# Gate/up products in five PSUM banks per unit, in another order, with operands moved to 64 modulo 256 bytes

## The chip, the cores and the metric

The kernel runs on one core of one Trainium2 chip. The metric is device time in microseconds (us). The core has a matmul engine (PE, with its weight loads shown as PEld), a vector engine (DVE), a scalar engine (ACT), GpSimd (POOL), and DMA queues, most of them fed by SyncE (SP). Each engine runs its own instructions in order. Matmul results go into PSUM, which has eight banks of 512 fp32 columns on 128 partitions; operands lie in SBUF.

## The reference

One encoder layer on a 1024 x 1024 activation in fp32: a half-step feed-forward network (FFN 1), two attention groups with 8 heads each, a second half-step FFN (FFN 2), and a final norm.

```python
def swiglu(h, w_gu, w_down):                      # w_gu 1024 x 5632, w_down 2816 x 1024
    a, b = jnp.split(h @ w_gu, 2, axis=-1)
    return (jax.nn.silu(a) * b) @ w_down

h = modulate(rms_norm(x, g_ffn1), sh_f1, sc_f1)
x = x + 0.5 * gt_f1 * swiglu(h, w1_gu, w1_down)   # FFN 1
h = modulate(rms_norm(x, g_mix), sh_m, sc_m)
z = h @ w_in                                      # then the two attention groups
x = x + gt_m * (concat(rms_norm(o_mla), rms_norm(o_gqa)) @ w_out)
h = modulate(rms_norm(x, g_ffn2), sh_f2, sc_f2)
x = x + 0.5 * gt_f2 * swiglu(h, w2_gu, w2_down)   # FFN 2
return rms_norm(x, g_final)
```

The shifts, scales and gates come from `silu(c) @ w_ada + b_ada`, nine blocks of 1024.

## The kernel before, in words

Every fp32 operand is split into two parts, high (`h`, rounded) and low (`l`, the remainder), and a product is three matmuls: high by high, low moving operand by high, high by low (lines 484 to 486). One matmul takes a stationary operand of 128 x 128 and a moving one of 128 x 512.

The gate/up product `h @ w_gu` of each FFN is done in 22 units. A unit is a 2 x 2 block product in which seven products stand for eight: A11 B11, A12 B21, S1 T1, S2 T2, S3 T3, S4 B22 and A22 T4. The A and S blocks are made from the weights and are the stationary operands; the B and T blocks are made from the activations, stay in SBUF for the whole stage (`B11h`, `T1l` and so on) and are the moving operands. A product is 12 matmuls (four blocks of depth by three). A profile row such as `ps<-T1h,uh` is the product S1 T1, `B22h` is S4 B22, `T4h` is A22 T4, `B21h` is A12 B21.

The weights come through a stream (class `Stream`, lines 52 to 159): a 1 MB DMA per unit into one of two `raw` buffers, POOL and DVE form S1 to S4 (line 424), then each block is split: ACT copies the high part (`uh`, line 105), DVE subtracts to get the low part (`ul`, line 106). A ring of nine split blocks runs ahead of the products. The order of the splits is the list of steps in `unit_specs`. After every product `tick()` lets the stream do two steps, and every second tick adds one step of the modulation sums (line 311: a DVE instruction on 1024 columns, fed by a 512 KB DMA; rows `acc<-ada,cact,acc`; FFN 1 only).

What follows a product is on DVE and ACT: U2 = A11 B11 + S2 T2 (line 629), U4 = U2 + S1 T1 (line 637), and `post` (lines 494 to 510), which adds what is missing, applies silu on even units, and multiplies on odd ones. POOL forms sums of the results (line 520), and they go to DRAM for the down product.

For units 0 to 7 ("early" units) A11 B11 and A12 B21 are done ahead, and A11 B11 comes back from DRAM as `c1`; only five products remain in `run()`. Units 8 to 21 have all seven.

`run()` takes its PSUM banks by `ps1()`, which goes round six banks in a fixed order (`SIX`). Before, a unit of seven products uses three: `bank[u]` for A11 and A12, `b` for S2, S1 and S4 one after the other, `c` for S3 and A22. S1 is added onto S2 in `b`, so PE may start S1 only when U2 has been read from `b`, and S4 only when U4 has been read. A22 is added onto S3 in `c` after `post(u, 1, 1)` has read `c`. The modulation stage takes banks from the same round: one for a set of columns (line 326), two for a gate (line 340).

A scheduler puts the instructions of each engine in order at build time from its own estimates, and may set matmuls of one product between those of another where it expects a wait.

SBUF is handed out in pools from the left and from the right end. On the right come `rawp`, `tmp`, `sm`, `sp` and then, in FFN 1, the pools R1 and R2 with the B and T blocks. On the left lie the constants, the ring, and in FFN 2 the pools R1b and R2b with the B and T blocks. With the sizes of the pools, the ring's tiles and those of R1b and R2b start at 64 modulo 256 bytes, those of `rawp` and `tmp` at 224, and those of `sp`, R1, R2 and the right-side tiles of the attention (K, Q, V, the probabilities, `hT`) at 96.

Of the kernel before, what the change touches and what calls it, by code (L numbers as in the profile page):

```python
# [15 lines left out]
F32 = mybir.dt.float32  # L16
# [3 lines left out]
ALU = mybir.AluOpType  # L20
# [4 lines left out]
P = 128  # L25
# [26 lines left out]
class Stream:  # L52
# [87 lines left out]
    def get(self, key):  # L140
        while key not in self.units:
            assert self.i <= self.where[key], key
            if self._next_is_block() and self.live >= RING:
                self.live -= self.freed
                self.freed = 0
                assert self.live < RING, key
            self._step()
        return self.units[key]
# [35 lines left out]
def encoder_layer(ctx: ExitStack, tc: tile.TileContext, a: dict, out: bass.AP):  # L184
    nc = tc.nc

    const = ctx.enter_context(tc.tile_pool(name="const", bufs=1))
    ring = ctx.enter_context(tc.tile_pool(name="ring", bufs=RING))
    rawp = ctx.enter_context(tc.tile_pool(name="rawp", bufs=RAWB, side="right"))
    tmp = ctx.enter_context(tc.tile_pool(name="tmp", bufs=6, side="right"))  # L190
    sm = ctx.enter_context(tc.tile_pool(name="sm", bufs=4, side="right"))
# [6 lines left out]
    def tick(n=2):  # L198
        bg.step()
        st.pump(n)  # L200
        ada_ticks[0] += 1
        if ada_ticks[0] % 2 == 0:
            ada.pump(1)
# [8 lines left out]
    def t2(name, dt=F32):  # L212
        return tmp.tile([P, 512], dt, tag="t2", name=name, bufs=6)

    def small(n, name):
        return sm.tile([P, 16], F32, tag="small", name=name, bufs=18)[:, 0:n]

    def mm3(o, ah, al, bh, bl, start, stop):
        nc.tensor.matmul(o, ah, bh, start=start, stop=False)
# [3 lines left out]
    def inv_rms(ss, dims, r):  # L223

        v = small(ss.shape[1], "v")
        if isinstance(dims, int):
            nc.vector.tensor_scalar(v, ss, 1.0 / dims, EPS, op0=ALU.mult, op1=ALU.add)  # L227
        else:
            for i, d in enumerate(dims):
                nc.vector.tensor_scalar(v[:, i:i + 1], ss[:, i:i + 1], 1.0 / d, EPS, op0=ALU.mult, op1=ALU.add)  # L230
        nc.gpsimd.tensor_tensor(r, v, neghalf[:, 0:ss.shape[1]], op=ALU.pow)  # L231
# [40 lines left out]
    def use_banks(kinds):  # L272
        banks.update(kinds=kinds, n=0, pair=None)

    def ps2():
        return p2p.tile([P, 1024], F32, tag="ps2", name="ps2")

    def ps1():

        if banks["pair"] is not None:  # L280
            p = banks["pair"][:, 512:1024]
            banks["pair"] = None
            return p
        kind = banks["kinds"][banks["n"] % len(banks["kinds"])]
        banks["n"] += 1
        if kind[0] == "2":
            p = ps2()
            if kind == "2":
                banks["pair"] = p
            return p[:, 0:512]  # L290
        return (p0p if kind == "0" else p1p).tile([P, 512], F32, tag="ps1", name="ps1")
# [62 lines left out]
    def norm_gen(t, xt, i, hTh=None, hTl=None, hf=None):  # L354

        ss = small(1, "ss")
        sumsq(xt, ss)
        yield
        r = small(1, "r")
        inv_rms(ss, D, r)  # L360
        yield
        xn = t4("xn")
        nc.vector.tensor_scalar(xn, xt, r, None, op0=ALU.mult)
        yield
        c, q = divmod(t, 4)
        qs = slice(q * P, (q + 1) * P)
        p = [ps1().rearrange("p (k q) -> p k q", k=4) for half in range(2)]
        for k in range(KT):
            nc.tensor.transpose(out=p[k // 4][:, k % 4, :], in_=xn[:, k * P:(k + 1) * P], identity=ident)
        h = hf[c][:, :, qs] if hf else t4("h").rearrange("p (k q) -> p k q", k=KT)  # L370
        for k in range(KT):
            nc.scalar.activation(h[:, k, :], p[k // 4][:, k % 4, :], AF.Identity,
                                 scale=modA[i][:, k:k + 1], bias=modB[i][:, k:k + 1])
        if hf:
            return
        yield
        dh = hTh[c][:, :, qs]
        dl = hTl[c][:, :, qs]
        nc.vector.tensor_copy(dh, h)
        nc.vector.tensor_tensor(dl, h, f32(dh), op=ALU.subtract)  # L380
# [33 lines left out]
    def unit_specs(i, u, early):  # L414

        src = a[f"w{i}_gu"][u // 2, u % 2]
        A = [slice(j * 512, (j + 1) * 512) for j in range(4)]
        tmps = {}

        def comb(nm, eng, x, y, op):  # L420
            def f(raw):
                tmps[nm] = sp.tile([P, 512], F32, tag="S", name="S")
                get = lambda v: tmps[v] if isinstance(v, str) else raw[:, A[v]]
                eng.tensor_tensor(tmps[nm], get(x), get(y), op=op)  # L424
            return f

        def blk(nm, v):
            if isinstance(v, str):
                return ((i, u, nm), None, lambda raw: tmps[v])
            return ((i, u, nm), A[v], None)  # L430

        direct = not early
        steps = [comb("S1", nc.gpsimd, 2, 3, ALU.add), comb("S3", nc.gpsimd, 0, 2, ALU.subtract)]
        if direct:
            steps.append(blk("A11", 0))
        steps += [comb("S2", nc.vector, "S1", 0, ALU.subtract), blk("S2", "S2")]
        if direct:
            steps.append(blk("A12", 1))
        steps += [blk("S1", "S1"), blk("S3", "S3"), comb("S4", nc.vector, 1, "S2", ALU.subtract), blk("S4", "S4"),
                  blk("A22", 3)]  # L440
        return [(src, steps)]

    gtp = {}
# [1 line left out]
    class GateUp:  # L445
# [164 lines left out]
        def run(self):  # L610
            use_banks(SIX)
            K4 = (0, 1, 2, 3)
            self.load_p1(0)
            for u in range(NU):
                early = u < NE
                self.load_p1(u + 1)
                if early and u % 2:
                    self.g["A21"] = gtp["g"]()
                    nc.sync.dma_start(self.g["A21"], ge_d[u // 2])
                if not early:  # L620
                    self.bank[u] = ps1()
                    self.prod(self.bank[u], u, "A11", "B11", K4, True, True)
                    self.keep_p1(u)
                    tick()
                c1 = self.c1.pop(u)
                b = ps1()
                self.prod(b, u, "S2", "T2", K4, True, True)
                u2 = t2("U2")
                nc.vector.tensor_tensor(u2, b, c1, op=ALU.add)
                tick()  # L630
                if not early:
                    self.prod(self.bank[u], u, "A12", "B21", K4, False, True)
                    self.post(u, 0, 0, self.bank[u])
                    tick()
                self.prod(b, u, "S1", "T1", K4, False, True)
                u4 = t2("U4")
                nc.vector.tensor_tensor(u4, b, c1, op=ALU.add)
                tick()
                c = ps1()
                self.prod(c, u, "S3", "T3", K4, True, True)  # L640
                self.post(u, 1, 1, c, u4)
                tick()
                self.prod(b, u, "S4", "B22", K4, False, True)
                self.post(u, 0, 1, b, c1)
                tick()
                self.prod(c, u, "A22", "T4", K4, False, True)
                self.post(u, 1, 0, c, u2)
                del self.bank[u]
                tick()

    def gu_specs(i):
        for u in range(NU):
            for src, steps in unit_specs(i, u, "rest" if u < NE else None):
                st.add(src, steps)
# [753 lines left out]
    for s in range(NQ + LAG + 3):  # L1408
# [5 lines left out]
        b = s - LAG  # L1414
        if 0 <= b < NQ:
            g, e = divmod(b, 2)
# [299 lines left out]
```

## Time and profile before

| | us |
|---|---|
| median of 3 runs (2076.69 to 2081.34) | 2081.32 |
| profiled execution | 2080.87 |
| its span, first to last instruction | 2079.1 |
| PE busy | 1989.1 (96%) |
| DVE busy | 1556.7 (75%) |
| ACT busy | 977.0 (47%) |
| POOL busy | 473.6 (23%) |

The stages lie in the span about like this: the start and the early products to 98 us, `run()` of FFN 1 to 537, its down product to 750, projections and attention to 1315, the output projection to 1417, early products and `run()` of FFN 2 to 1859, its down product to the end. A matmul's row shows a duration of about 0.39 us, but matmuls overlap: the pace is the distance from one start to the next. A wait stands in brackets behind the instruction that waited, with its releaser.

### The profile page before, as it was taken

Reading aid. Unit: us, or ns where it says so; the run is one execution under the profiler, and the core shown is the slowest. Engines: PE = TensorE matmul, PEld = TensorE weight load, DVE = VectorE, ACT = ScalarE, POOL = GpSimd, SP = SyncE. Lnnn points to the kernel's source line nnn. Section 1 sums busy time; section 2 is a strip of 40 time slices with the busy share of each in tenths; the row PEclk is TensorE's granted clock in tenths of the full one; section 3 lists DMA queues with packets and bytes.
Section 4 is the critical chain, followed back from the end, with each engine's and each line's share of the span. In section 5 each row is a group of like instructions: output and inputs, shape, how many; then the busy total and the mean of one; then the engine's idle time right before and its main releaser. Section 6 shows DMA issues by size and latency. Waiting matters only on the chain. (4 is left out here: it accounts for less than half of the span.)

```text
span 2079.1 us, 28011 instructions
## 1 busy us (share of the span) xinstructions
PE 1989.1 (96%) x10301; PEld 1678.2 (81%) x10301; DVE 1556.7 (75%) x2381; ACT 977.0 (47%) x1865; POOL 473.6 (23%) x428
## 2 busy tenths in 40 slices
PE   6889999999999999899999999998899999999998
PEld 4667777777788888888989999997678888888886
DVE  7898777775598777588788877776877566656976
ACT  6522222223344473477787777466332333234444
POOL 1533433332100014121220000014444233220011
PEclk9899999999999999999999999999999999999999
DMA  8266654542752342631343332243453233268223
GB/s 339 104 236 202 203 166 157 190 155 101 296 221 92 122 145 90 175 117 58 111 147 102 82 82 62 102 142 127 147 176 136 78 126 103 80 225 332 96 92 117
DMA packets 90550, 303.30 MB, mean 146 GB/s; under 512 B 9848, under 2 KB 22427, under 8 KB 76588
## 3 DMA queue, kind: packets, MB, share of 16 engines
q1 hardware_dynamic: 81018, 274.21, 39.4%
q0 software_dynamic: 7040, 23.07, 2.8%
q10 hardware_dynamic: 2354, 4.22, 0.5%
q8 instruction: 81, 1.33, 0.3%
q14 instruction: 57, 0.47, 0.1%
HBM read 220.98 MB, written 80.49 MB: 145 GB/s over the span
## 5 line engine op out<-in xcount | busy, mean ns | idle before, releaser
L106 DVE TENSOR_TENSOR ul<-raw,uh 128x512 fp32r<-128x512 f32 (+1 forms) x343 | 275.6, 810 | 68.2 <-ACT uh L105 68.0
L105 ACT CAST uh<-raw 128x512 fp32r<-128x512 f32 (+1 forms) x343 | 210.5, 622 | 236.3 <-PE ps L485 165.0
L105 ACT CAST uh<-S 128x512 fp32r<-128x512 f32 x198 | 122.0, 622 | 369.7 <-PE ps L485 277.9
L726 PE MATMUL ps<-uh 128*128 128x512 f32 x616 | 240.6, 391 | 1.1 <-ACT uh L105 1.0
L727 PE MATMUL ps<-ul,uh 128*128 128x512 f32 x616 | 240.2, 390 | 0.6 <-DVE ul L106 0.6
L728 PE MATMUL ps<-uh,ul 128*128 128x512 f32 x616 | 240.0, 390 | 0.0
L1413 DVE TENSOR_REDUCE nm<-ps 128x1 f32<-128x1024 f32 x128 | 155.6, 1215 | 70.3 <-PE ps L221 40.9
L424 POOL TENSOR_TENSOR S<-raw 128x512 f32<-128x512 f32 x88 | 125.7, 1434 | 290.8 <-DVE ul L106 138.9
L106 DVE TENSOR_TENSOR ul<-S,uh 128x512 fp32r<-128x512 f32 x198 | 168.9, 857 | 30.4 <-ACT uh L105 27.6
L520 POOL TENSOR_TENSOR g<-g 128x512 f32<-128x512 f32 x88 | 125.1, 1421 | 221.0 <-DVE g L507 219.6
L1431 ACT CAST ph<-ps 128x512 fp32r<-128x512 f32 x256 | 138.0, 590 | 79.5 <-PE ps L1430 79.3
L1441 DVE TENSOR_TENSOR pl<-ps,ph 128x512 fp32r<-128x512 f32 x256 | 163.9, 682 | 0.0
L1436 ACT ACTIVATE pe<-ps,nm 128x1024 f32<-128x1024 f32 x128 | 143.7, 1123 | 17.0 <-DVE nm L1413 17.0
L726 PEld LDWEIGHTS ps<-uh 128*128 128x128 f32 x616 | 115.7, 188 | 25.9 <-ACT uh L105 2.0
L727 PEld LDWEIGHTS ps<-ul,uh 128*128 128x128 f32 x616 | 115.7, 188 | 25.0 <-DVE ul L106 1.2
L1430 PE MATMUL ps<-ident,pe 128*128 128x128 f32 x1024 | 134.8, 273 | 0.8 <-DVE pl L1441 0.4
L728 PEld LDWEIGHTS ps<-uh,ul 128*128 128x128 f32 x616 | 115.7, 188 | 23.8
L1430 PEld LDWEIGHTS ps<-ident,pe 128*128 128x128 f32 x1024 | 119.6, 140 | 18.9 <-DVE pl L1441 0.6
L1379 PE MATMUL po<-ph,V 128*128 128x256 f32 x512 | 129.5, 291 | 0.0
L1380 PE MATMUL po<-pl,V 128*128 128x256 f32 x512 | 125.7, 284 | 0.0
L105 ACT CAST uh<-hT 128x512 fp32r<-128x512 f32 x96 | 59.7, 622 | 137.4 <-PE ps L727 102.3
L231 POOL TENSOR_TENSOR r<-v,neghalf 128x1 f32<-128x1 f32 x32 | 25.9, 810 | 358.0 <-DVE v L227 358.0
(282 smaller groups left out, 5190.1 us busy)
## 6 DMA issues: line engine op xcount, KB each, us to landing
raw<-in_w_gu_dram SPq DMA_DIRECT2D x52, 1024.0 KB, 4.9
ada<-in_w_ada_dram SPq DMA_DIRECT2D x56, 512.0 KB, 3.6
g_S<-g POOLq DMA_DIRECT2D x88, 256.0 KB, 2.6
g_A<-g SPq DMA_DIRECT2D x66, 256.0 KB, 3.6
hT<-in_w_down_dram SPq DMA_DIRECT2D x16, 1024.0 KB, 10.3
raw<-g_S SPq DMA_DIRECT2D x16, 1024.0 KB, 4.8
raw<-g_A SPq DMA_DIRECT2D x12, 1024.0 KB, 5.0
x<-in_x_dram SPq DMA_DIRECT2D x16, 512.0 KB, 14.9
```

Of the source, the lines that this page charges most:

```text
L105: nc.scalar.copy(hi[:, 0:n], ap)
L106: nc.vector.tensor_tensor(lo[:, 0:n], ap, f32(hi[:, 0:n]), op=ALU.subtract)
L424: eng.tensor_tensor(tmps[nm], get(x), get(y), op=op)
L726: nc.tensor.matmul(p, gh[:, tsl], wh, start=start, stop=False, skip_group_check=True)
L727: nc.tensor.matmul(p, gh[:, tsl], wl, start=False, stop=False, skip_group_check=True)
L728: nc.tensor.matmul(p, gl[:, tsl], wh, start=False, stop=stop, skip_group_check=True)
L1379: nc.tensor.matmul(po[:, 0:256], V, gr.ph[:, k, :], start=(k == 0), stop=False)
L1413: nc.vector.tensor_reduce(nm, p, axis=AX.X, op=ALU.max, negate=True)
L1430: nc.tensor.transpose(out=pt[:, k, :], in_=pe[:, (4 * n + k) * P:(4 * n + k + 1) * P], identity=ident)
L1431: nc.scalar.copy(gr.ph[:, 4 * n:4 * n + 4, es], pt)
L1436: nc.scalar.activation(pe, p, AF.Exp, bias=nm, accum_out=ls[:, s % 2:s % 2 + 1])
L1441: nc.vector.tensor_tensor(gr.pl[:, nsl, es], pts[n], f32(gr.ph[:, nsl, es]), op=ALU.subtract)
```

## The change

1. In `run()` S1, S2 and S4 get a bank each (`e`, `b`, `d`), so a unit of seven uses five banks: `bank[u]` (A11, A12), `b` (S2), `e` (S1), `c` (S3, A22), `d` (S4). U4 is now `e` + U2, and the result of S4 is `d` + U4.
2. The order of the products becomes A11, S2, S1, S3, A12, S4, A22; before it was A11, S2, A12, S1, S3, S4, A22. The splits in `unit_specs` follow. Early units have S2, S1, S3, S4, A22 in both.
3. A pad of 160 bytes at the right end (`padr`, 40 fp32) and two more `small` buffers of 64 bytes. With these the right-side pools `rawp` and `tmp` move by 160 bytes, and `sp` and all behind it by 288. So every SBUF operand of a product starts at 64 modulo 256: 224 - 160 = 64, and 96 - 288 + 256 = 64. The left side stays.

```diff
+    padr = ctx.enter_context(tc.tile_pool(name="padr", bufs=1, side="right"))
+    padr.tile([P, 40], F32, name="padr")
     rawp = ctx.enter_context(tc.tile_pool(name="rawp", bufs=RAWB, side="right"))
...
-        return sm.tile([P, 16], F32, tag="small", name=name, bufs=18)[:, 0:n]
+        return sm.tile([P, 16], F32, tag="small", name=name, bufs=20)[:, 0:n]
...
-        steps += [comb("S2", nc.vector, "S1", 0, ALU.subtract), blk("S2", "S2")]
+        steps += [comb("S2", nc.vector, "S1", 0, ALU.subtract), blk("S2", "S2"), blk("S1", "S1"), blk("S3", "S3")]
         if direct:
             steps.append(blk("A12", 1))
-        steps += [blk("S1", "S1"), blk("S3", "S3"), comb("S4", nc.vector, 1, "S2", ALU.subtract), blk("S4", "S4"),
-                  blk("A22", 3)]
+        steps += [comb("S4", nc.vector, 1, "S2", ALU.subtract), blk("S4", "S4"), blk("A22", 3)]
...
-                if not early:
-                    self.prod(self.bank[u], u, "A12", "B21", K4, False, True)
-                    self.post(u, 0, 0, self.bank[u])
-                    tick()
-                self.prod(b, u, "S1", "T1", K4, False, True)
+                e = ps1()
+                self.prod(e, u, "S1", "T1", K4, True, True)
                 u4 = t2("U4")
-                nc.vector.tensor_tensor(u4, b, c1, op=ALU.add)
+                nc.vector.tensor_tensor(u4, e, u2, op=ALU.add)
                 tick()
                 c = ps1()
                 self.prod(c, u, "S3", "T3", K4, True, True)
                 self.post(u, 1, 1, c, u4)
                 tick()
-                self.prod(b, u, "S4", "B22", K4, False, True)
-                self.post(u, 0, 1, b, c1)
+                if not early:
+                    self.prod(self.bank[u], u, "A12", "B21", K4, False, True)
+                    self.post(u, 0, 0, self.bank[u])
+                    tick()
+                d = ps1()
+                self.prod(d, u, "S4", "B22", K4, True, True)
+                self.post(u, 0, 1, d, u4)
                 tick()
                 self.prod(c, u, "A22", "T4", K4, False, True)
                 self.post(u, 1, 0, c, u2)
```

On PE, at unit 7 (an early one) of FFN 1, before: the end of S2 T2 (into bank `ps_1772`), then the first four matmuls of S3 T3 (into `ps_1814`), then S1 T1, again into `ps_1772`.

```order
L486 MATMUL ps_1772<-T2h_568,ul 128x512
L484 MATMUL ps_1772<-T2h_568,uh 128x512
L485 MATMUL ps_1772<-T2l_569,uh 128x512
L486 MATMUL ps_1772<-T2h_568,ul 128x512
L484 MATMUL ps_1814<-T3h_560,uh 128x512
L485 MATMUL ps_1814<-T3l_561,uh 128x512
L486 MATMUL ps_1814<-T3h_560,ul 128x512
L484 MATMUL ps_1814<-T3h_560,uh 128x512
L484 MATMUL ps_1772<-T1h_556,uh 128x512
```

The same place now: S2 T2 goes into `ps_1790`, S1 T1 into a bank of its own, `ps_1812`.

```order
L485 MATMUL ps_1790<-T2h_572,uh 128x512
L486 MATMUL ps_1790<-T2l_573,uh 128x512
L487 MATMUL ps_1790<-T2h_572,ul 128x512
L485 MATMUL ps_1812<-T1h_560,uh 128x512
L486 MATMUL ps_1812<-T1l_561,uh 128x512
L487 MATMUL ps_1812<-T1h_560,ul 128x512
```

S1 stands directly behind S2, the part of S3 that had been set between them is gone, and the two write to different banks.

On DVE, at unit 11 (odd, with seven products) of FFN 1, before: U2, a result of A12 (line 507 on a PSUM bank), U4, and the result of S3 (line 506 with U4).

```order
L629 TENSOR_TENSOR U_2414<-ps_2401,c_2390 128x512
L106 TENSOR_TENSOR ul<-S,uh 128x512
L507 TENSOR_TENSOR g<-ps_2377,s 128x512
L106 TENSOR_TENSOR ul<-S,uh 128x512
L424 TENSOR_TENSOR S<-S,raw 128x512
L637 TENSOR_TENSOR U_2453<-ps_2401,c_2390 128x512
L106 TENSOR_TENSOR ul<-S,uh 128x512
L424 TENSOR_TENSOR S<-raw,S 128x512
L506 TENSOR_TENSOR g<-ps_2461,U_2453 128x512
```

The same unit now, to the result of A12 (`ps_2403`).

```order
L630 TENSOR_TENSOR U_2440<-ps_2427,c_2416 128x512
L106 TENSOR_TENSOR ul<-S,uh 128x512
L426 TENSOR_TENSOR S<-S,raw 128x512
L635 TENSOR_TENSOR U_2459<-ps_2446,U_2440 128x512
L106 TENSOR_TENSOR ul<-raw,uh 128x512
L507 TENSOR_TENSOR g<-ps_2468,U_2459 128x512
L106 TENSOR_TENSOR ul<-S,uh 128x512
L508 TENSOR_TENSOR g<-g,s 128x512
L426 TENSOR_TENSOR S<-raw,S 128x512
L508 TENSOR_TENSOR g<-ps_2403,s 128x512
```

DVE does the same kinds of instruction; U4 reads its own bank and U2, and the result of A12 comes behind that of S3.

## Rows read from the trace of the kernel before

**Rows 1.** The page, busy time of two engines: us, share of span, instructions.

```profile
PE 1989.1 (96%) x10301; PEld 1678.2 (81%) x10301; DVE 1556.7 (75%) x2381; ACT 977.0 (47%) x1865; POOL 473.6 (23%) x428
```

**Rows 2.** Windows: start:end, length, then busy time of each engine (instructions), clock, DMA.

```profile
core 0: us, PE busy (x) PEld busy (x) DVE busy (x) ACT busy (x) POOL busy (x), PEclk, DMA share, GB/s
98.40:237.60 139.20, 126.48 (x516) 98.84 (x515) 118.18 (x138) 37.31 (x63) 53.36 (x45) 0.95 0.65 215
237.60:470.00 232.40, 220.04 (x945) 173.86 (x944) 181.71 (x209) 65.74 (x110) 83.20 (x74) 0.99 0.52 173
470.00:537.00 67.00, 67.00 (x289) 53.88 (x288) 33.48 (x51) 20.13 (x34) 10.32 (x11) 1.00 0.36 133
1600.00:1700.00 100.00, 100.00 (x443) 82.83 (x442) 61.38 (x84) 32.61 (x54) 31.18 (x29) 1.00 0.27 95
```

**Rows 3.** PE's waits, 98.4 to 237.6: us in total, times, longest.

```profile
PE ps L484 <- DVE U L629: 7.1, 4, 3.2
PE ps L484 <- DVE U L637: 5.2, 2, 3.5
```

**Rows 4.** PE's waits, 237.6 to 470 (all that there are).

```profile
PE ps L484 <- DVE U L637: 7.1, 5, 3.4
PE ps L484 <- DVE U L629: 5.3, 5, 1.7
```

**Rows 5.** Timeline about one wait: start, us, engine, line, operation, tiles.

```profile
291.77 4.16 DVE L311 SCALAR_TENSOR_TENSOR acc<-ada,cact,acc 128x1024 f32<-128x1024 f32 x1
292.28 1.31 POOL L520 TENSOR_TENSOR g<-g 128x512 f32<-128x512 f32 x1
293.53 1.30 POOL L424 TENSOR_TENSOR S<-raw 128x512 f32<-128x512 f32 x1
...
298.25 0.68 DVE L637 TENSOR_TENSOR U<-ps,c 128x512 f32<-128x512 f32 x1
298.98 0.65 PE L484 MATMUL ps<-B22h,uh 128*128 128x512 f32 x1 [3.36 <-DVE U L637]
301.54 0.68 DVE L500 TENSOR_TENSOR s<-ps,U 128x512 f32<-128x512 f32 x1
```

**Rows 6.** Timeline of PE, first and last of gapless stretches in FFN 1.

```profile
472.65 0.40 PE L484 MATMUL ps<-B22h,uh 128*128 128x512 f32 x1
...
534.25 0.40 PE L484 MATMUL ps<-T4h,uh 128*128 128x512 f32 x1
```

**Rows 7.** The same for FFN 2.

```profile
1605.81 0.39 PE L484 MATMUL ps<-B22h,uh 128*128 128x512 f32 x1
...
1796.21 0.39 PE L484 MATMUL ps<-B22h,uh 128*128 128x512 f32 x1
```

**Rows 8.** The same for the input projection, 512 columns.

```profile
787.34 0.40 PE L219 MATMUL ps<-uh,hT 128*128 128x512 f32 x1
...
792.94 0.40 PE L219 MATMUL ps<-uh,hT 128*128 128x512 f32 x1
```

**Rows 9.** DVE groups by line, 98.4 to 237.6: count, busy us, mean ns, idle before.

```profile
L106 DVE TENSOR_TENSOR ul<-S,uh 128x512 fp32r<-128x512 f32 x36 | 30.0, 847 | 0.0
```

**Rows 10.** PE's waits, 1466 to 1592.3, `run()` of FFN 2, early units.

```profile
PE ps L484 <- ACT es L501: 1.8, 1, 1.8
PE ps L484 <- DVE U L629: 1.5, 3, 0.6
```

**Rows 11.** Timeline of PE: scores of one step, and what follows them.

```profile
1216.25 0.40 PE L219 MATMUL ps<-K,Q 96*128 96x512 f32 x1
...
1217.64 0.60 PE L1430 MATMUL ps<-ident,pe 128*128 128x128 f32 x4
```

**Rows 12.** Timeline of PE: probabilities by V, first and last of 13.

```profile
1214.57 0.28 PE L1379 MATMUL po<-ph,V 128*128 128x256 f32 x1
...
1216.01 0.28 PE L1379 MATMUL po<-ph,V 128*128 128x256 f32 x1
```

**Rows 13.** Timeline of PE: output projection, `oth` from the left side, 25 starts.

```profile
1356.57 0.28 PE L219 MATMUL ps<-uh,oth 128*128 128x256 f32 x1
...
1359.45 0.28 PE L219 MATMUL ps<-uh,oth 128*128 128x256 f32 x1
```

## The prediction

> **What bounds the kernel now.** I read the page first. PE is busy 1989.1 of 2079.1 us, DVE 1556.7 [rows 1], so the kernel is paced by PE nearly everywhere, and time can be won in two ways only: matmuls that start closer together, or PE pauses that go. The profiled execution took 2080.87 us, 1.8 us more than its span and 0.45 us less than the median of the runs, so a sum made on it needs no correction.
>
> The windows then show where PE pauses [rows 2]. `run()` of FFN 1 has three stretches. In A, 98.4 to 237.6 us (early units), PE is busy 126.5 of 139.2 us at a mean clock of 0.95. In B, 237.6 to 470, it is 220.0 of 232.4 us at 0.99. In C, 470 to 537, PE is busy throughout, as in the late units of FFN 2 (the window 1600 to 1700). The table of PE's waits gives the cause: in A 7.1 us for U2 (line 629) and 5.2 us for U4 (line 637) [rows 3]; in B 7.1 us for U4 and 5.3 us for U2, and nothing else [rows 4]. These are the two reads of the shared bank `b`. They come where the modulation sums run beside the units: one such sum took 4.16 us while POOL worked, U4 came at 298.25, and S4 waited 3.36 us for it [rows 5]. DVE is busy 118.2 of 139.2 us in A and 181.7 of 232.4 us in B, but 33.5 of 67 us in C [rows 2], where the sums are over.
>
> The third view is the timeline of starts in gapless stretches. In FFN 1, 264 matmuls from 472.65 to 534.25 us make 61.60 / 264 = 233.3 ns from start to start [rows 6]. In FFN 2, 840 from 1605.81 to 1796.21 us make 190.40 / 840 = 226.7 ns [rows 7]. Clock 1.00, shape, line and stationary operand are the same in both; what differs is where the B and T blocks lie: at 96 modulo 256 on the right in FFN 1, at 64 on the left in FFN 2. In the input projection the moving operand (ring) is at 64 and the stationary one (`hT`, right side) at 96: 24 matmuls in 5.60 us, 233.3 ns again [rows 8]. I read this as 6.7 ns per matmul of 512 columns as soon as one of its operands starts at 96.
>
> **The change part by part.** *Operands at 64.* `run()` of FFN 1 has 8 x 60 + 14 x 84 = 480 + 1176 matmuls. The 1176 of B and C save 1176 x 6.67 ns = 7.8 us. Those of A are worth 3.2 us but stand beside a loaded DVE, so they are counted with A below. The 192 early products are worth at most 1.3 us; PE pauses much there, so 0.5. The input projection has 192 matmuls of 512 columns: 1.3 us. The scores have 640 of 512 columns, both operands at 96: six, up to the next instruction, take 1.39 us or 232 ns [rows 11], so 0 to 3.4 us; I take half, 1.7, because the nearest other pair in that stage shows nothing: probabilities by V, 256 columns with both at 96, keep 120 ns [rows 12], and the output projection with both at 64 has 2.88 us / 24 = 120 ns too [rows 13]. Everything else of fewer columns is taken at nothing, with 2 us to either side. FFN 2 and both down products have their operands at 64 already: nothing.
>
> [...] The rows on the starts differ by 6.7 ns, and only the run can say whether by start or by side.
>
> *S1 and S4 in banks of their own, stretch B.* The waits of 7.1 and 5.3 us have no reason left: neither S1 nor S4 touches a bank that was read a moment ago. The slow restart behind a wait goes with them: the mean clock of 0.99 over 232.4 us is 2.3 us. What is late next is A22, which must still find `c` read by `post(u, 1, 1)`. That comes behind U4 on DVE, but in a unit of seven two products (A12, S4, together 5.4 us) now lie between S3 and A22, where before one did. In the worst case of the trace U4 started at 298.25 and the read of `c` at 301.54, done at 302.2 [rows 5]; S3 had ended about 295.6, so A22 would come at 301.0 and wait 1.2 us in place of 3.36. Two such cases make 2 us left. The gate of the modulation takes two banks of the round of six; with five per unit, `d` then falls on `bank[u]`, and S4 waits for the result of A12 just done. By the order this happens twice in B; DVE reads such a bank in 0.68 us [rows 5] behind one or two others, so about 1 us each, 2 us (0 to 5). B and C together: 7.8 + 12.4 + 2.3 - 2 - 2 = 18.5 us saved (13 to 22.5).
>
> *Stretch A.* The early units have no A12 between S2 and S1, so before S1 waits for U2 in any case; now it follows at once. But DVE becomes the limit: it is busy 118.2 us there [rows 2], with 36 splits of S blocks at 847 ns [rows 9] where an undisturbed DVE instruction of this size takes 0.68 us [rows 5]. The change takes nothing from DVE (U4 reads one bank and one SBUF tile, as before). PE's own work is 516 x 0.2267 = 117 us. So A can't fall below about 120 us, and two engines that are both nearly full, with only S4 between S3 and A22 as slack, do not reach that. I take 127, a gain of 12 us, between 3 (only the alignment comes through) and 19.
>
> [...]
>
> *FFN 2, early units.* U2 is waited for 1.5 us, and ACT 1.8 us [rows 10]; the latter stays. With the restarts I take 2 us (1 to 3).
>
> *More splits in another order.* The steps of the stream follow the products, the same number on the same engines; the ring keeps its lead of nine blocks, which hides it (PE waits for no split in A and B [rows 3, 4]). If that lead were used up, PE would wait for `ul`, up to 0.85 us a block.
>
> Sum: 18.5 (B, C) + 12 (A) + 2 (FFN 2) + 1.3 (input projection) + 1.7 (scores) + 0.5 (early products) = 36.0 us. 2080.87 - 36.0 = 2044.9, so 2045.
>
> **The rivals.** *First: it is the side, not the start.* In the trace all operands at 96 lie in right-side pools and all of FFN 2's at 64 on the left, so the 6.7 ns may belong to the place or to something of FFN 1. Then the pad buys nothing: B and C lose 7.8, A some 3, and 3.5 of projection, scores and early products go: 36.0 - 14.3 = 21.7 us, 2059. For it: both pools of 96 are on the right, and the scores, with both operands at 96, run no slower than those with one. Against it: in the input projection it is the other operand that lies at 96, and the pace is the same to 0.1 ns.
>
> *Second: the waits move to A22.* DVE is late by the same amount, and PE meets it one or two products further on. Then A keeps only its 3 us, B and C keep 7.8 and a third of 14.7, FFN 2 has 1, the rest 3.5: 20 us, 2061. For it: in A the slack is one product, and DVE is 85% busy. Against it: A22 does not appear among the waits now, and in B its slack doubles.
>
> *Third, slower: A22 waits in every unit.* `post(u, 1, 1)` stands behind U4 and up to three splits and combinations on DVE; were it late by over 5.4 us (2.7 in early units) in all 44 units of both FFNs, A22 would wait each time. The gain is eaten when that wait is 36.0 / 44 = 0.8 us a unit on average; at 1.2 us it makes 2098. Against it: in FFN 2's late units and in C nothing waits at all, with less slack.
>
> *Fourth: hardly any effect*, if the alignment is the side's and DVE paces all of A and B as before: 2077 or so.
>
> **How the numbers follow.** The forecast has 0.57, with a range of its own of 2030 to 2058: A at 120, B and C at 22.5, the scores at 3.4 and the small ones at their best give 51 us or 2030; A at 132 (7), B and C at 13, FFN 2 at 1 and the scores at 0 give 23 us or 2058. The first rival has 0.2, the second 0.15, the third 0.03, the fourth 0.05. The range of 2028 to 2066 takes in the first two, and 2 us for the matmuls of fewer columns. A measurement of this kernel tells 0.3%, 6.2 us, from no change: faster by more has 0.57 + 0.2 + 0.15 = 0.92, within has 0.05, slower 0.03.
>
> **What would show it.** Right: starts 226.7 ns apart in FFN 1's `run()` and in the input projection's 512-column part, no wait for U2 or U4 left in the table of PE's waits, A near 127 us with DVE over 90% busy, a few waits on the read of `c` (tile `T4h`) or of `bank[u]` (tile `B22h`) in A and B. Wrong: 233 ns in FFN 1 (first rival); `T4h` waits that sum to ten us or more (second); PE pauses in FFN 2's late units, where there are none (third); or slower matmuls of 128 or 256 columns in the attention.

## The result, and the profile after

The changed kernel took 2058.15 us (median of 4 runs, 2051.58 to 2059.17), the kernel before on the same chip 2081.33 (2076.69 to 2083.57). The ratio is 0.9881, 95% interval 0.9870 to 0.9893: faster, by 23 us where 36 were forecast. The span of the profiled execution is 2056.6 us against 2079.1. By stage, each from its first matmul to the first of the next; FFN 2's early products (51.8 and 51.7 us) and the 2.7 us of transpositions between attention and output projection are left out:

| stage | before, us | after, us | difference | forecast |
|---|---|---|---|---|
| FFN 1, early products | 74.7 | 73.5 | -1.2 | -0.5 |
| FFN 1, `run()`, stretch A | 138.9 | 132.0 | -6.9 | -12 |
| FFN 1, `run()`, B and C | 299.4 | 279.7 | -19.7 | -18.5 |
| FFN 1, down product | 216.9 | 220.6 | +3.8 | 0 |
| input projection | 123.8 | 121.7 | -2.1 | -1.3 |
| attention | 434.2 | 434.5 | +0.3 | -1.7 |
| output projection | 102.8 | 103.7 | +0.8 | 0 |
| FFN 2, `run()` | 389.5 | 386.7 | -2.8 | -2 |
| FFN 2, down product | 220.3 | 225.9 | +5.6 | 0 |

The windows of the same three stretches, which answer to [rows 2]; the columns are the same:

```profile
97.30:229.30 132.00, 121.81 (x512) 98.11 (x513) 119.74 (x137) 37.37 (x63) 54.12 (x44) 0.95 0.65 219
229.30:442.00 212.70, 210.37 (x943) 172.76 (x943) 179.00 (x210) 62.51 (x108) 81.34 (x71) 1.00 0.56 190
442.00:509.00 67.00, 66.73 (x292) 54.40 (x290) 31.83 (x46) 17.94 (x32) 13.97 (x15) 1.00 0.31 113
```

In B, PE now pauses 2.3 us in place of 12.4, and DVE's share rose to 84%. In A, DVE is busy 119.7 of 132 us, as long as before: the stretch became shorter and DVE had the same to do.

PE's waits in A, and below the dots all of those in B, answer to [rows 3, 4]: us in total, times, longest.

```profile
PE ps L485 <- DVE s L501: 9.4, 3, 5.0
PE ps L485 <- POOL acc L310: 3.5, 1, 3.5
PE ps L485 <- DVE g L507: 0.7, 1, 0.7
...
PE ps L485 <- DVE s L501: 1.8, 3, 1.0
PE ps L485 <- DVE g L507: 0.5, 1, 0.5
```

No wait for U2 or U4 is left. The one for `acc` is the pause ahead of the first product of `run()` (S2 T2, begun at 97.32 us) and is over before A begins. That GpSimd ended it is not certain: the splits of that product were made in the same microsecond. All the others are at A22 (`T4h`), at the reads of `c`, most of them at `s` of line 501, the read by `post(u, 1, 1)`, which A22 must follow. They sum to 12.4 us, 10.1 of them in A, where PE's pauses thus fell from 12.7 only to 10.2 us; the rest of A's gain, 4.4 us, is PE's own busy time. The longest of these waits in the timeline, to be laid beside [rows 5]:

```profile
142.74 2.77 DVE L313 SCALAR_TENSOR_TENSOR acc<-ada,cact,acc 128x1024 f32<-128x1024 f32 x1
...
145.43 0.68 DVE L635 TENSOR_TENSOR U<-ps,U 128x512 f32<-128x512 f32 x1
...
146.03 0.68 DVE L106 TENSOR_TENSOR ul<-S,uh 128x512 fp32r<-128x512 f32 x1
146.63 0.68 DVE L426 TENSOR_TENSOR S<-raw,S 128x512 f32<-128x512 f32 x1
147.23 0.68 DVE L501 TENSOR_TENSOR s<-ps,U 128x512 f32<-128x512 f32 x1
...
148.06 0.76 PE L485 MATMUL ps<-T4h,uh 128*128 128x512 f32 x1 [5.00 <-DVE s L501]
```

A modulation sum of 2.77 us, then U4, a split, a combination, and only then the read of `c`; A22 (`T4h`) stood for 5.0 us. It is the case of [rows 5], with another product at its end.

The starts in FFN 1 without a gap, which answer to [rows 6]:

```profile
448.73 0.39 PE L485 MATMUL ps<-T4h,uh 128*128 128x512 f32 x1
...
472.30 0.39 PE L487 MATMUL ps<-B11h,ul 128*128 128x512 f32 x1
```

The two starts are 104 matmuls apart: 23.57 us / 104 = 226.6 ns, where there were 233.3. In the input projection's 512-column part, the starts without a gap are 227.2 ns apart on the mean, against 233.3.

The new loss lies at the head of both down products. SyncE's queue there, before (the first four rows) and after:

```profile
526.04 0.81 SPq L714 DMA_DIRECT2D hT<-in_w_down_dram  x2
...
540.47 0.39 SPq L95 DMA_DIRECT2D raw<-g_A  x1
...
553.56 0.32 SPq L395 DMA_DIRECT2D gate<-gd  x1
...
556.05 0.98 SPq L95 DMA_DIRECT2D raw<-g_A  x2
```

```profile
502.06 0.32 SPq L517 DMA_DIRECT2D g_A<-g  x1
503.32 0.81 SPq L717 DMA_DIRECT2D hT<-in_w_down_dram  x2
...
521.41 0.33 SPq L397 DMA_DIRECT2D gate<-gd  x1
521.78 1.95 SPq L978 DMA_DIRECT2D x<-in_x_dram  x4
523.84 0.97 SPq L95 DMA_DIRECT2D raw<-g_A  x2
```

The down product starts at 537.05 before and at 509.04 after. Its first `w_down` load went out 11.0 us ahead of it, and now 5.7. The third chunk of `g_A12` (`raw`) went out 3.4 us behind its start, ahead of the gate row; now it goes 14.8 us behind, after the gate row (which waits 9.3 us for the last `g_S` store to leave its place) and four loads of x. ACT and PE then show the price (after):

```profile
532.92 0.62 ACT L105 CAST uh<-raw 128x512 fp32r<-128x512 f32 x1 [11.18 <-DMA raw<-g_A]
```

```profile
534.11 0.50 PE L729 MATMUL ps<-uh 128*128 128x512 f32 x1 [1.92 <-ACT uh L105]
534.92 0.50 PE L730 MATMUL ps<-ul,uh 128*128 128x512 f32 x1 [0.31 <-DVE ul L106]
...
1857.19 0.79 PE L729 MATMUL ps<-uh 128*128 128x512 f32 x1 [3.31 <-ACT uh L105]
```

```profile
531.00:541.00 10.00, 7.77 (x26) 5.67 (x25) 6.80 (x11) 5.92 (x11) 0.00 (x0) 0.83 0.91 350
1853.00:1863.00 10.00, 6.68 (x22) 4.74 (x22) 6.12 (x10) 5.92 (x11) 0.00 (x0) 0.83 0.82 319
```

PE stands for 1.9 and 3.3 us, and the mean granted clock over these ten us is 0.83; windows of one us show 0.50 from 537 to 539 and from 1858 to 1860, and 1.00 from 540 and from 1861 on. Added up over the starts of each stretch, what exceeds 227 ns a matmul is 4.4 and 5.5 us, so pause, late second operand and lower clock together cost more than the pause. Another 1.2 us go in the first five us of each down product. The first down product of before has a pause of its own, 1.9 us with its restart, at 568 us.

### The profile page after: what moved, and what is told of

It reads as the page before. It is cut to its first block, busy times and chain, and to the rows that moved or that the text cites. A ratio compares the mean times of both kernels' runs of the same rounds, so it can differ in the third digit from the quotient of the medians.

```text
span 2056.6 us, 28024 instructions
## 1 busy us (share of the span) xinstructions
PE 1974.8 (96%) x10301; PEld 1678.4 (82%) x10301; DVE 1570.0 (76%) x2381; ACT 973.6 (47%) x1865; POOL 473.5 (23%) x428
## 5 line engine op out<-in xcount | busy, mean ns | idle before, releaser
L106 DVE TENSOR_TENSOR ul<-raw,uh 128x512 fp32r<-128x512 f32 (+1 forms) x343 | 255.0, 749 | 42.6 <-ACT uh L105 42.3
L106 DVE TENSOR_TENSOR ul<-S,uh 128x512 fp32r<-128x512 f32 x198 | 193.7, 982 | 46.0 <-ACT uh L105 42.9
L521 POOL TENSOR_TENSOR g<-g 128x512 f32<-128x512 f32 x88 | 124.8, 1418 | 227.2 <-DVE g L508 226.3
L1433 PEld LDWEIGHTS ps<-ident,pe 128*128 128x128 f32 x1024 | 119.7, 141 | 19.0 <-DVE pl L1444 0.6
```

Source lines behind the costliest of these rows:

```text
L106: nc.vector.tensor_tensor(lo[:, 0:n], ap, f32(hi[:, 0:n]), op=ALU.subtract)
L1433: nc.tensor.transpose(out=pt[:, k, :], in_=pe[:, (4 * n + k) * P:(4 * n + k + 1) * P], identity=ident)
```

## The experiments

Stage lengths are from one profiled execution each. `run()` of FFN 1 in kernels whose code there is the same came out between 408.6 and 411.9 us, so less than 3 us in it is not told apart.

**The alignment alone (e1).** The kernel before, with the pad and the two `small` buffers of the change:

```diff
+    padr = ctx.enter_context(tc.tile_pool(name="padr", bufs=1, side="right"))
+    padr.tile([P, 40], F32, name="padr")
-        return sm.tile([P, 16], F32, tag="small", name=name, bufs=18)[:, 0:n]
+        return sm.tile([P, 16], F32, tag="small", name=name, bufs=20)[:, 0:n]
```

> The kernel before with the 160-byte pad and 20 small tiles alone: banks, products and splits as before, operands of FFN 1 at 64. Theory (start, not side, and the two halves of the change add up): starts 226.7 ns apart in FFN 1's run(), the waits for U2 and U4 stay at about 25 us there, run() of FFN 1 goes from 438.4 to about 428 us, input projection 1.9 us less, both down products as before (216.9 and 220.3): 2068 us in the profile. Rival A (the waits swallow it: DVE sets the pace wherever PE waits, so faster products only wait longer): only the stretches without waits gain, run() at 434, total 2075. Rival B (it was the changed banks or order, not the start, that made the starts 226.7): nothing changes, 2079.

Measured: 2076.39 us, ratio 0.9974 (0.9963 to 0.9986). The starts are 226.7 ns apart, but `run()` only went from 438.4 to 434.5 us: rival A. The table of PE's waits over the whole span shows why, before above the dots and e1 below them:

```profile
PE ps L484 <- DVE U L629: 13.8, 12, 3.2
PE ps L484 <- DVE U L637: 12.3, 7, 3.5
...
PE ps L486 <- DVE U L631: 15.2, 11, 3.7
PE ps L486 <- DVE U L639: 13.7, 6, 3.9
```

Where DVE's result ended the wait, the faster products only waited longer: 28.9 us in the two rows of e1, 26.1 in those of before.

**Banks and order alone (e2).** The changed kernel without the pad and the two buffers.

> The changed kernel without the pad and with 18 small tiles: banks and order new, operands of FFN 1 at 96 as before. Theory (the parts add up): starts 233.3 ns apart, no wait for U2 or U4, run() of FFN 1 at about 421 us (411.7 plus 1656 matmuls x 6.67 ns = 11, less what then hides late DVE work), both down products as slow as in the changed kernel (220.6 and 225.9), total about 2069. Rival (order and banks bring nearly all, DVE being the limit in the first half): run() at 414, total 2061.

Measured: 2064.59 us, ratio 0.9920 (0.9903 to 0.9937); `run()` 416.3 us at 233.3 ns, no wait of PE at all in B and C, both down products slow (220.1 and 224.5). The two halves add up, as far as the intervals tell: 5.7 us (e1) and 17.5 (e2) of the median before, 23.2 together. `run()` lies between the rival's 414 and the theory's 421: of the 11 us of pace about 5 come through (416.3 against 411.7), and B and C have pauses again in the changed kernel, 2.6 us where e2 has none.

**The last unit in the old order (e3).** The changed kernel, with A12 B21 of unit 21 back behind S2, in products (shown) and in splits:

```diff
+                if u == NU - 1:
+                    self.prod(self.bank[u], u, "A12", "B21", K4, False, True)
+                    self.post(u, 0, 0, self.bank[u])
+                    tick()
                 e = ps1()
...
-                if not early:
+                if not early and u < NU - 1:
                     self.prod(self.bank[u], u, "A12", "B21", K4, False, True)
```

> The changed kernel, but in the last unit of each FFN A12 B21 stands behind S2 again, in products and splits. Theory (the down products lost 3.8 and 5.6 us because the last unit reads B21 two products later: the first load of w_down goes into B21's place and waits for that read, so the first splits of the down product begin 5.7 instead of 11 us ahead of it, and the gate and x loads then come ahead of the third g_A12 chunk): down products back at 217 and 220.5, run() unchanged at 411.7 and 386.7, total 2047.5. Rival (the down products lose because PE reaches them faster or because the last post comes later, whatever the last unit's order): down products stay at 220.6 and 225.9, total 2056.6.

Measured: 2048.24 us, ratio 0.9848 (0.9827 to 0.9870). Down products 217.1 and 221.5. SyncE's queue is that of before again; the down product starts at 507.06:

```profile
496.37 0.81 SPq L724 DMA_DIRECT2D hT<-in_w_down_dram  x2
...
511.26 0.84 SPq L95 DMA_DIRECT2D raw<-g_A  x1
...
524.04 0.32 SPq L397 DMA_DIRECT2D gate<-gd  x1
```

One product moved in one unit of each FFN makes most of the loss: 7.9 of 9.4 us come back.

**The place of the first load (e4).** The changed kernel, with B tiles allocated name by name, so that the load falls into B11's place alone:

```diff
-            for k2 in range(2):
-                for nm in names:
+            for nm in names:
+                for k2 in range(2):
```

> The changed kernel with the B and T tiles laid out by name, so that the first load of w_down goes into the place of B11 alone (last read by the unit's first product) and not half into B21's. The queue of SP keeps its order: the load stands behind the store of the last A12 result, which DVE gives about 7 us ahead of the down product. Theory 1 (both the place and the store hold it, 1.2 us apart): the load is issued about 1 us sooner, the down products gain 0 to 1.5 us each, total 2055. Theory 2 (only the place holds it): the load goes out 5 us or more sooner, down products back at 217 and 220.5, total 2047.5. Theory 3 (neither): 2056.6 and nothing moves in the queue.

Measured: 2058.20 us, ratio 0.9890 (0.9870 to 0.9910), down products 221.1 and 225.6. The load went out 6.1 us ahead of the down product, not 5.7. SyncE's own waits there:

```profile
SPq L517 <- DVE g L508: 21.0, 3, 16.1
...
SPq L717 <- PE ps L487: 1.7, 2, 0.9
```

The load still waited 0.9 us for PE behind that store, so the edit did not free it from PE, and the store of the last A12 result ahead of it held it nearly as long. Nothing moved clear of noise, which is theory 3 and the lower end of theory 1; theory 2 is not tested by it, and whether the place alone decides stays open.

**The gate row from another queue (e6).** The changed kernel, gate row and four loads of x of both down products issued by GpSimd (the first down product is shown):

```diff
-    gate = bcast_row(dp, gd[0], "gate")
+    gate = bcast_row(dp, gd[0], "gate", nc.gpsimd)
...
-    x_load(range(4, 8))
+    x_load(range(4, 8), nc.gpsimd)
```

> The changed kernel with the gate row and four x loads of both down products issued by GpSimd in place of SyncE, so that the third chunk of g_A12 no longer stands behind the gate row, which waits 9.3 us. Theory (two stalls make the loss: 0.7 + 1.4 us at the start of the down product from the late first load of w_down, and 2.7 us with a slow restart behind it from the late third chunk): the second goes, the first stays; down products at 218 and 222, total 2050. Rival (the third chunk is late because its buffer is freed late, not because of what stands ahead of it): down products stay at 220.6 and 225.9, 2056.6.

Measured: 2046.96 us, ratio 0.9834 (0.9820 to 0.9848). Down products 216.2 and 220.6, better than expected. The `w_down` load is as late as in the changed kernel (501.44, for a start at 507.12), yet PE's waits there are small, and the third chunk (the first of the two loads of the first row) waits for its buffer alone and goes 7.0 us behind the start:

```profile
514.07 6.26 SPq L95 DMA_DIRECT2D raw<-g_A  x2
...
PE ps L730 <- DVE ul L106: 0.5, 1, 0.5
PE ps L729 <- ACT uh L105: 0.3, 1, 0.3
```

So the second of the two stalls, the third chunk's, made the loss. The first stays, 1.2 us at the head of the first down product, and is made up for by the pause of before at 568 us, which e6 does not have. Late `w_down` load and third chunk behind the gate row came together in every kernel with the new last unit and SyncE's gate row; that the one brings the other is likely, but no run parts them.

**Banks and order apart (e5, e10).** e5 is the changed kernel with A12 B21 behind S2 in every unit; e10 has the new order with the shared bank:

```diff
-                e = ps1()
-                self.prod(e, u, "S1", "T1", K4, True, True)
+                self.prod(b, u, "S1", "T1", K4, False, True)
...
-                nc.vector.tensor_tensor(u4, e, u2, op=ALU.add)
+                nc.vector.tensor_tensor(u4, b, c1, op=ALU.add)
...
-                d = ps1()
-                self.prod(d, u, "S4", "B22", K4, True, True)
-                self.post(u, 0, 1, d, u4)
+                self.prod(b, u, "S4", "B22", K4, False, True)
+                self.post(u, 0, 1, b, c1)
```

> The changed kernel with its private banks and its pad, but with products and splits in the order of before (A12 behind S2 in every unit). Theory 1 (the banks take the waits away; the order gives A22 its slack): the down products are back at 217 and 221, but with S4 alone between S3 and A22 the waits for the read of c, 1.7 us behind unit 8 in the changed kernel, grow by 3 to 5 us; run() of FFN 1 at 411 to 413, since the last unit's order brought it to 408.3; total 2049 to 2052. Theory 2 (the banks do all of it, the order nothing): run() at 408.3, total 2046.5 as with the last unit alone in the old order. Theory 3 (the order did it: with U2 read while A12 runs, PE waits for U2 or S1 again): run() at 425 or more, total 2063.

> The changed kernel's order of products and splits and its pad, with the shared bank b of before (S2, S1 and S4 in one bank, U4 from b and c1). Theory 1 (bank and order need each other): S1 now follows S2 at once in every unit and waits for the read U2 in each, 1.0 us or more in 44 units with the restart; S4 has two products between and waits no more; run() of FFN 1 at 430 to 445, FFN 2's at 400 to 420, the down products as slow as in the changed kernel: total 2090 to 2120. Theory 2 (the order is what brings the gain, the banks little, as the old order with the new banks kept 425.5 of run()): run() at 412 to 418, total 2060.

Measured: e5 2066.94 us, ratio 0.9923 (0.9910 to 0.9937), `run()` 425.5; e10 2102.49 us, ratio 1.0117 (1.0099 to 1.0135), slower than before, `run()` 440.3 and in FFN 2 394.8. Largest of PE's waits in `run()` of FFN 1, e5 and then e10:

```profile
PE ps L485 <- DVE s L501: 21.6, 7, 5.5
```

```profile
PE ps L485 <- DVE U L630: 24.4, 10, 7.2
PE ps L485 <- DVE U L634: 5.0, 3, 3.6
```

With the pad in all four, `run()` is 434.5 (both old), 425.5 (new banks), 440.3 (new order), 409.0 to 411.9 (both). In e5 the wait moved to A22, the mechanism of theory 1: of the 21.6 us 11.0 are in A and 10.6 behind it, where theory 1 had 5 to 7 and the changed kernel has 1.8. The time is that of theory 3, but the waits for U2 or S1 that it named are not there. In e10 S1 follows the read U2 at once and waits for it, in 10 of the 22 units by the table; FFN 2, at 394.8, came out below theory 1's 400 to 420. Neither half does it alone: the private banks take away two waits, and A12 between S3 and A22 covers most of the one that takes their place.

**Fewer modulation sums in A (e7).** The kernel of e3, with `ada.pump` at every fourth tick in the early units:

```diff
+                ada_every[0] = 4 if early else 2
...
-        if ada_ticks[0] % 2 == 0:
+        if ada_ticks[0] % ada_every[0] == 0:
```

> The kernel of e3 (last unit in the old order), with the modulation sums run at every fourth tick in the early units of FFN 1 and at every second behind them as before; about ten of the 21 sums of stretch A (1474 ns each) move into the units behind it. Theory (DVE, 91% busy, sets the end of A): DVE has 15 us less to do there, the waits for the read of c in A (9.9 us) fall below 4, A goes from 133 to about 126 us; the units behind it run with sums to their end and lose at most 2 us; run() of FFN 1 at 403, total 2041. Rival (A is set by the start-up: the first loads, the splits and ACT, whatever the sums): A stays within 2 us, total 2046.

Measured: 2042.08 us, ratio 0.9811 (0.9793 to 0.9829); A from 130.3 to 124.4 us, `run()` 402.0. The windows to 226 us (A and 2 us more) and from there to the end of `run()`:

```profile
99.50:226.00 126.50, 118.34 (x507) 95.86 (x506) 108.23 (x129) 36.78 (x62) 54.25 (x44) 0.97 0.59 206
226.00:501.00 275.00, 275.00 (x1238) 227.35 (x1237) 224.20 (x267) 83.71 (x143) 95.61 (x84) 1.00 0.56 192
```

DVE is busy 108 us in the first window, in e3 120 to the end of A, and behind it PE runs without a pause. The rival, by which A would stay within 2 us, falls. But the theory's sign did not come: the waits for the read of `c` in A fell from 9.9 to 7.8 us, not below 4, and one of them is 6.2 us long. Of the 5.9 us, 1.7 are 16 one-column matmuls of a modulation, which now run behind A. DVE's load is shown as one cause of A's length; what the waits left in A hang on stays open.

**Matmuls alone (e8).** 72 matmuls in a group, no other work beside them:

> Matmuls alone, nothing of the layer computed: groups of 72 with 512 columns (hi, lo, and the next stationary block, as in the products), the moving operand at 0, 16, 32, 48, 64, 80, 96, 112, 128, 160, 192 and 224 modulo 256 and the stationary one at 64; then the stationary one at 0, 32, 96 and 128 with the moving one at 64; both at 96; and four groups of 256 columns with each at 64 or 96. Theory 1 (a start that is no multiple of 64 costs): 226.7 ns at 0, 64, 128, 192, and 233.3 at 16, 32, 48, 80, 96, 112, 160, 224, in either operand; 256 columns nowhere. Theory 2 (only starts in the second half of a 64-byte piece, as 96, 32, 160, 224 and beyond, cost): 16, 80 stay at 226.7. Theory 3 (not the start, but the load of the rest of the kernel or the side): 226.7 everywhere.

The first matmul of each group, in the timeline of PE; `mov` and `stat` carry the start modulo 256 of the moving and the stationary operand, `w` is 512 columns and `n` 256:

```profile
17.37 0.39 PE L57 MATMUL p<-mov0w,stat64w 128*128 128x512 f32 x1
34.17 0.40 PE L57 MATMUL p<-mov16w,stat64w 128*128 128x512 f32 x1
...
84.18 0.40 PE L57 MATMUL p<-mov64w,stat64w 128*128 128x512 f32 x1
100.54 0.39 PE L57 MATMUL p<-mov80w,stat64w 128*128 128x512 f32 x1
...
251.38 0.39 PE L57 MATMUL p<-mov64w,stat96w 128*128 128x512 f32 x1
268.18 0.40 PE L57 MATMUL p<-mov64w,stat128w 128*128 128x512 f32 x1
284.97 0.40 PE L57 MATMUL p<-mov96w,stat96w 128*128 128x512 f32 x1
301.34 0.28 PE L57 MATMUL p<-mov64n,stat64w 128*128 128x256 f32 x1
309.98 0.28 PE L57 MATMUL p<-mov96n,stat64w 128*128 128x256 f32 x1
318.46 0.28 PE L57 MATMUL p<-mov64n,stat96w 128*128 128x256 f32 x1
```

Each difference over 72 is the pace of the group: 0 with 64 is 16.80 / 72 = 233 ns; 64 with 64 is 16.36 / 72 = 227; 64 with 96 is 233; **96 with 96 is 16.37 / 72 = 227**. With 256 columns it is the other way: 8.64 / 72 = 120 ns alike, 8.48 / 72 = 118 unlike. None of the three theories holds: both starts count, against each other. The two pairs, 64 with 64 and 96 with 96, are the only alike ones tried. With the stationary operand at 64, a moving one at 48 gave 226.8 ns, 128 gave 229.0, 80 gave 231.6, and 16, 32, 96, 112, 160, 192 and 224 gave 233 to 235; why 48 is fast stays open.

**Everything at 96 (e9).** The changed kernel without the pad on the right, with 32 bytes ahead of the ring on the left:

```diff
+    padl = ctx.enter_context(tc.tile_pool(name="padl", bufs=1))
+    padl.tile([P, 8], F32, name="padl")
     ring = ctx.enter_context(tc.tile_pool(name="ring", bufs=RING))
```

> The changed kernel without the pad on the right and with 18 small tiles (so the B and T blocks of FFN 1 lie at 96 again), but with 32 bytes ahead of the ring of splits on the left, which puts the ring and all of FFN 2's blocks at 96 too: no operand of the products lies at 64 any more, and both operands of each pair lie alike. Theory 1 (what counts is whether the two operands start alike, as in the group of matmuls with both at 96, 227.2 ns): 226.7 ns apart in FFN 1, FFN 2, both down products and the input projection, total as the changed kernel, 2057 to 2058. Theory 2 (the start at 64 itself, as the prediction had it): 233.3 ns in all of them; FFN 1's run() back at 416, FFN 2's and both down products (1848 matmuls of splits by splits among them) 6.7 ns a matmul slower, 12 us in each pair of stages, total about 2085.

Measured: 2058.73 us, ratio 0.9903 (0.9886 to 0.9920), and 226.7 ns in FFN 1, FFN 2 and both down products: theory 1. In this kernel it is not the start at 64, but that the two operands start alike.

**Together (e11, e12).** e11 is e7 with the gate row's move of e6, e12 the changed kernel with that move and e7's sums.

> Three changes together: last unit in the old order, gate row and four x loads of the down products from GpSimd, modulation sums at every fourth tick in the early units. Theory 1 (the first two mend the same loss: each alone brought the down products to 217 and 221, 216 and 220.6): run() at 402, down products at 215.6 and 220.3, total 2039, as without the gate's move (2042.1 in the median). Theory 2 (they add up, the first from the late w_down, the second from the late third chunk): 2 us more each, 2037.

> The changed kernel with the gate row and four x loads from GpSimd and the modulation sums at every fourth tick in the early units, its own order kept in the last unit. Theory 1 (the gate's move alone mends the down products): down products at 216.2 and 220.6, run() at 402 to 403, total 2039 to 2041. Theory 2 (with the late w_down load left, the down products keep the first stall once the units before it are faster): down products at 217.5 and 222, total 2043.

Measured: e11 2040.07 us, ratio 0.9813 (0.9796 to 0.9829), down products 214.9 and 219.4; e12 2043.21 us, ratio 0.9827 (0.9811 to 0.9844), 216.6 and 220.6. e11's time is theory 1's, and its down products lie about halfway between the two theories: the two cures add something, but not 2 us each. e12 has the down products and the `run()` (402.9) of theory 1 and the time of theory 2; its early products took 75.8 us, 2.0 more than e11's, which is the spread of that stage. e7 and e11 have the lowest times; between them no difference is shown.

## Why the prediction was right, and where it was wrong

- **The time: right, in part by luck.** 2058.15 us lies at the edge of the forecast's own range (2030 to 2058), and the first two rivals (2059 and 2061) come nearer to it than 2045. Only starts and waits tell them apart. Starts at 226.6 ns rule out the first rival; B and C, which gained all they were given, speak against the second; in A and by the prediction's own sign (`T4h` waits of ten us or more, measured 12.4) the second was right.
- **B and C, 18.5 us: right** (19.7). U2 and U4 are gone as waits, and 2.3 us are left at A22 where 2 were put. S4 behind A12 in the same bank, put at 2 us, does not appear among the waits.
- **Start, not side: right against its rival, wrong as a rule.** FFN 1 has 226.6 ns with its operands still on the right, so the first rival falls. But the step "as soon as one of its operands starts at 96" named one operand where the runs show the pair (e8, e9). So the scores, with both operands at 96 before and both at 64 after, gained nothing of the 1.7 us given them; that they stay at 231 ns with an equal pair is open. The output projection lost 0.8: 480 of its 256-column matmuls (five of its eight row blocks, on the right) had unlike starts before, and went from about 118 to 120 ns. Rows 12 and 13 of before had shown the equal pair at both starts, and the prediction took them to show nothing.
- **The alignment, 14.3 us in the sum: mis-sized.** The pace came as forecast, the time did not: alone it brought 5.7 us (e1), and beside banks and order about as much (2064.59 to 2058.15). Where DVE's result ended a wait, the faster products waited longer (28.9 us in e1, 26.1 before).
- **A, 12 us: the step was mis-sized** (6.9). DVE's load was right (119.7 us busy, put at 118.2). The waits did what the second rival said: they moved to the read of `c`, because only S4 lies between S3 and A22 in early units, and of 12.7 us of pauses 10.2 stayed. e7 shows DVE's load as one cause.
- **"The ring keeps its lead of nine blocks": right in `run()`, wrong behind it**, and with it the down products, put at nothing. The lead was read from A and B; the last unit was not followed into the next stage. With A12 B21 two products later the first `w_down` load goes 5.3 us later and the third `g_A12` chunk stands behind the gate row on SyncE; both down products together lost 9.4 us. e3 and e6 each give most or all of it back. With the last unit alone put back the kernel took 2048.2 us, 3.2 us above the forecast.
- **FFN 2, 2 us, the input projection, 1.3, and early products, 0.5: right** within a microsecond (2.8, 2.1, 1.2). Of the 2.1, 0.8 came without the pad too (e2), and the 1.2 means little: kernels with the same code there took 73.5 to 75.7 us.
- **The third rival** (A22 waits everywhere) did not come: `T4h` waits 8 times in FFN 1 and never in FFN 2. e5 shows what it hung on: with S4 alone between S3 and A22, the wait for `c` behind A is 10.6 us in place of 1.8.

## What to carry to other kernels

When an order of work is changed in a loop, follow its last pass into the next stage: which buffer is now read last, which load waits for that read, and what moves ahead of what on that load's queue. A wait that goes is worth only what the next wait on the same engine leaves: here the private banks alone brought 9 us of `run()`, the order alone cost 6, and both together brought some 24. Read the starts of both operands of a matmul, not of one.

## What the runs showed of the hardware

- Matmuls of 512 columns started 227 ns apart with both operands at 64, or both at 96, modulo 256 bytes (e8). With 64 under one operand and another start under the other it was mostly 233; a moving operand at 48 (227), 128 (229) or 80 (232) came nearer (e8). With 256 columns alike was slower, 120 ns against 118 (e8).
- Behind pauses of PE of 1.9 and 3.3 us in the down products the granted clock was 0.83 over ten us, with 0.50 in single windows of one us, and these stretches lost 4.4 and 5.5 us in all.
- Modulation sums, DVE instructions on 1024 columns, took 1.27 us at the shortest and up to 5.1 us (56 of them in the changed kernel).
